# One layer of a streaming encoder on one core: the second copy of the band keys' upper half goes by DMA, and the last norm of the band rows stands behind two gate projections

## The chip, the core and the metric

The kernel runs on one core of one Trainium2 chip. The core has five engines, each with its own stream of instructions: TensorE (PE in the profile, with its weight loads as PEld), VectorE (DVE), ScalarE (ACT), GpSimd (POOL) and SyncE (SP), which here does nothing but issue DMAs. Engines wait for each other by semaphores. Matrix products are summed in PSUM, a small memory that PE writes and that DVE and ACT read out; all else lies in SBUF, a memory of 128 partitions, or in DRAM.

The metric is the device time of one execution, in microseconds (us). Lower is better.

## The reference

One layer is applied to a prompt of 1024 tokens and, with the same weights, to a sample of 32 tokens that has a cache of 512 older keys and values and a recurrent state. The change touches two things: how the keys of the band attention (branch B) are laid out before its scores, and when the last of its rows are divided by their softmax sums.

```python
h = rms_norm(x, g_pre_mix)
qa, ka, va, ra, alr, qb, kb, vb, ga, gb = split_cols(h @ w_in)
oa, s_gla = gla_branch(qa, ka, va, ra, alr, w_a2, b_a2, g_gla, gla_s0, gla_block)   # 4 linear heads
ob, k_rows, v_rows = attn_fn(qb, kb, vb, rel_bias)                                  # 8 band heads of 64
mix = (jax.nn.sigmoid(ga) * (oa @ w_br_a) + jax.nn.sigmoid(gb) * (ob @ w_br_b)) @ w_out
x = x + rms_norm(mix, g_post_mix)
f, conv_new = conv_ffn(rms_norm(x, g_pre_ffn), conv_s0, w_up, conv_w, conv_b, w_down)
x = x + rms_norm(f, g_post_ffn)
gate = jax.nn.sigmoid(rms_norm(x, g_pre_ple) @ w_ple_gate)
x = x + rms_norm(gate * (pe @ w_ple), g_post_ple)

def band_attend(q, k, v, q_pos, k_pos, rel_bias):
    s = jnp.einsum('bqhe,bkhe->bhqk', q, k).astype(jnp.float32) * HD_B ** -0.5
    ...
    s = jnp.where(vis, s + bias, -jnp.inf)
    p = jax.nn.softmax(s, axis=-1)
    return jnp.einsum('bhqk,bkhe->bqhe', p.astype(v.dtype), v)
```

## The kernel before

Activations are kept transposed: 128 features on the partitions, the 1056 tokens (prompt and sample together, `T`) along the free axis, cut into three chunks of 352. Everything is float32, but the products run on a rounded type (fp32r): each operand x is split into a rounded part (hi) and the rest (lo), and `product` adds three matmuls for each block of 128 features, hi weights by hi rows, hi weights by lo rows, lo weights by hi rows (L229, L230, L231). With eight blocks that makes 24 matmuls of 128 x 352 for one chunk of one projection.

**Weights.** `weights` loads 128 x 1024 numbers by one DMA on SP's queue (L199, tile `raw`, two buffers), ACT rounds each half (L208, `whi`, four buffers), and POOL subtracts (L209, `wlo`, four buffers). `project(n, evac)` loads one such block, runs the 24 matmuls for each of the three chunks in a PSUM tile `mm` (three buffers) and lets DVE read it out with the row scale (`to_tile`, L460). Full rows of 1056 go to tiles named `ev`, of which there are five for the whole kernel.

**Band attention.** The loop at L655 runs over four pairs of heads (`hp`). `band_project` projects Q, K and V of the pair, stores K and V, transposes V on PE (L505 and L510) and splits it. `band_head` then prepares one head of the two. A head has 64 features, and its q and k lie on partitions 0 to 63 or 64 to 127 of the pair's tile: `r` are the partitions it has, `o` the other 64. The score needs (q_hi + q_lo) by (k_hi + k_lo). The kernel does it with two matmuls over 128 partitions: `qs` holds q_hi on `r` and q_lo on `o`, `kh` holds k_hi on both halves and `kl` holds k_lo on both. So the halves `r` of `kh` and `kl` are made by ACT (L523, rounding) and DVE (L524, the rest), first for the 1056 new keys (`kf`), then for the 512 cached keys (`kc`), and each is then copied to the partitions `o` by L529: `kh` by POOL (`KHC` is 2) and `kl` by DVE (`KLC` is 0), 64 x 1568 numbers a copy. `probs` runs the two matmuls (L543 with `kh`, L544 with `kl`, PSUM tile `two`, one buffer), DVE adds the bias and finds the maximum (L550), ACT takes the exponential. The probabilities are transposed on PE (L559), split, and multiplied by V. The scores are written at high priority, so that the scheduler sets them ahead of projections.

After a pair its sums are inverted and stored to DRAM (`d_inv`, L678), the unnormed output rows too (`d_ob`, L684), and one projection of merge gates follows for pairs 0 to 2 (`gates`, which projects, takes the sigmoid and stores, L641).

**Norm.** `band_norm(hp)` loads the rows of a pair (L649), loads each head's inverses to 64 partitions (two DMAs, L651), multiplies on POOL (L652, 128 x 1056) and stores the result (L653). All four DMAs are on SP's queue. For pairs 0 to 2 it runs one pair later. For pair 3 it is called at L890, in the loop over the four linear heads.

**Linear heads.** `gla_project(h)` projects r, v, v, q, k of head 0, and q, k, v, v, r of the others. `gla_head` takes the decay of each token: a small product, ACT's exponentials, and nine scans on DVE (L786) over 128 tokens each. For each segment of 256 tokens DVE and ACT make seven scaled copies of q and k in a tile `x` (L807 is one of its operations), PE multiplies them (L835, PSUM tile `two`), DVE picks out the scores with masks (L840, L841), and PE applies them (L849). Then `gates(GLA_GATES[h])` projects two gates for head 0, 3, 2 and 6 for the others. The calls read

```python
for h in range(4):
    q, k, vt = gla_project(h)
    gla_head(h, q, k, vt)
    if h == 0:
        band_norm(3)
    gates(GLA_GATES[h])
```

**Order.** The code above is not the order in which the engines run it. The program is handed to a scheduler that plays the instructions through a timeline of its own and fixes for each engine the row in which they stand; what comes earlier in the code goes first where both could run, except for what is written at high priority (`weights`, the read-outs, the scores). Between such pieces, partial sums of the down weights (`d_s`, L430 on POOL's queue, L432 on SP's) are set in step by step. On each engine and in each DMA queue the instructions then run in that fixed row, and one that waits holds up all behind it.

Of the kernel before, what the change touches and what calls it, by code (L numbers as in the profile page):

```python
# [11 lines left out]
F32 = mybir.dt.float32  # L12
F32R = mybir.dt.float32r
U8 = mybir.dt.uint8
AF = mybir.ActivationFunctionType
ALU = mybir.AluOpType
# [6 lines left out]
T = NP + NS  # L23
# [34 lines left out]
GLA_GATES = (2, 3, 2, 6)  # L58
# [10 lines left out]
DVE_LO = (5,)  # L69
DVE_LO_O = (1, 3, 5, 7)  # L70
QSL = 2
KLL = 0
KLC = 0
NORM = 2
NORME = 0
KHC = 2
PSL = None
LOW_N = 50
LOW_G = 0
# [30 lines left out]
def emit(tc, a):  # L110
    nc = tc.nc
    ve, ac, po, pe, dma = nc.vector, nc.scalar, nc.gpsimd, nc.tensor, nc.sync
    uid = [0]
    E3 = (ve, ac, po)
# [5 lines left out]
    def pool(name, bufs=1, side="left"):  # L120
        return tc.alloc_tile_pool(name=name, bufs=bufs, side=side, reuse_waits="tile")

    def tl(p, shape, dt=F32, tag=None, bufs=None):
        tag = tag or nm("t")
        kw = {} if bufs is None else {"bufs": bufs}
        return p.tile(list(shape), dt, name=nm(tag), tag=tag, **kw)
# [31 lines left out]
    def evt():  # L158
        return tl(ev, [P, T], tag="ev", bufs=EVB)
# [287 lines left out]
    def project(n, evac):  # L447
        projects[0] += 1
        if projects[0] > 6:
            next(sums_left, None)  # L450
        hi, lo = weights(a["w_in"][n])
        for c in range(NC):
            s = chunk(c)
            ps = ps_mm()[:, : s.stop - s.start]
            product(ps, hi, lo, [(k, k) for k in range(KT)], lambda k: xh[:, k, s], lambda k: xl[:, k, s])
            with tc.high_priority():
                evac(ps, s)

    def to_tile(t):
        return lambda ps, s: ve.tensor_tensor(t[:, s], ps, rstd(s), op=ALU.mult)  # L460
# [54 lines left out]
    def band_head(hp, hd, qf, kf, kc, split, vs, ob, sums):  # L515
        r = slice(64 * hd, 64 * hd + 64)
        o = slice(64 - 64 * hd, 128 - 64 * hd)
        qs, kh, kl = split
        ac.activation(qs[r], qf[r], AF.Copy)
        E3[QSL].tensor_tensor(qs[o], qf[r], qs[r], op=ALU.subtract)  # L520

        for part, src in ((slice(0, T), kf), (slice(T, T + 512), kc)):
            ac.activation(kh[r, part], src[r], AF.Copy)  # L523
            E3[KLL].tensor_tensor(kl[r, part], src[r], kh[r, part], op=ALU.subtract)  # L524
        for e, t in ((KHC, kh), (KLC, kl)):
            if e == 1:
                ac.activation(t[o], t[r], AF.Copy)
            else:
                E3[e].tensor_copy(t[o], t[r])  # L529
        bias = tl(bp, [P, NS + 640], tag="bias", bufs=2)  # L530
        dma.dma_start(bias, a["rel"][2 * hp + hd])
        po.memset(bias[64:128, NS : NS + 64], NEG)
# [103 lines left out]
    def gates(cnt):  # L636
        for n, w0, dst in todo_gates[:cnt]:
            g = evt()
            project(w0 + n, to_tile(g))
            ac.activation(g, g, AF.Sigmoid)  # L640
            dma.dma_start(dst[n], g)  # L641
        del todo_gates[:cnt]
# [4 lines left out]
    def band_norm(hp):  # L647
        t, rb = evt(), evt()
        dma.dma_start(t, d_ob[hp])  # L649
        for hd in range(2):  # L650
            dma.dma_start(rb[64 * hd : 64 * hd + 64], d_inv[hp, hd, :T].partition_broadcast(64))  # L651
        po.tensor_tensor(t, t, rb, op=ALU.mult)  # L652
        dma.dma_start(d_on[hp], t)  # L653

    for hp in range(4):  # L655
        qf, kf, kc, split, vs = band_project(hp)
# [5 lines left out]
        for hd in range(2):  # L662
            po.memset(sums[hd], 1.0)
            work += band_head(hp, hd, qf, kf, kc, split[hd], vs, ob, sums[hd])
# [63 lines left out]
    def gla_project(h):  # L728
        q = tl(gp, [P, T], tag="qk", bufs=4)
        k = tl(gp, [P, T], tag="qk", bufs=4)  # L730
        vt = tl(gp, [P, 9, 256], tag="vt", bufs=2)
        vf = []
        for part in (ORD0 if h == 0 else ORD):
            if part == "q":
                project(Q0 + h, lambda ps, s: ve.scalar_tensor_tensor(q[:, s], ps, float(P ** -0.5), rstd(s), op0=ALU.mult, op1=ALU.mult))
            elif part == "k":
                project(K0 + h, to_tile(k))
            elif part == "r":
                gla_rest(h)
            elif part == "v":  # L740
                vf.append(evt())
                project(V0 + 2 * h + len(vf) - 1, to_tile(vf[-1]))
        for n in range(0, 9, 2):
            cnt = min(2, 9 - n)
            ps = ps_one()
            w = P if n < 8 else NS
            for i in range(cnt):
                for j in range(2):
                    pe.transpose(ps[:w, i * 256 + j * P : i * 256 + (j + 1) * P], vf[j][:, (n + i) * P : (n + i) * P + w], ident)
            ac.activation(vt[:w, n : n + cnt], ps[:w, : cnt * 256].rearrange("p (i v) -> p i v", v=256), AF.Copy)  # L750
        if 'r' not in (ORD0 if h == 0 else ORD):
            gla_rest(h)
        return q, k, vt
# [132 lines left out]
    for h in range(4):  # L886
        q, k, vt = gla_project(h)
        gla_head(h, q, k, vt)
        if h == 0:
            band_norm(3)  # L890
        gates(GLA_GATES[h])
    C0 = CHUNKS[0][1]
    b0 = [tl(gp, [P, 9 * 256], F32R, tag="vt", bufs=2)[:, : 4 * C0].rearrange("p (k t) -> p k t", t=C0)]
    b0 += [tl(gp, [P, T], F32R, tag="qk", bufs=4)[:, : 2 * C0].rearrange("p (k t) -> p k t", t=C0) for i in range(2)]
# [42 lines left out]
    op = pool("op")  # L937
    oa = [[tl(op, [P, T], F32R, tag=f"oa{kt}{x}") for x in "hl"] for kt in range(KT)]
    for kt in range(KT):
        t = evt()  # L940
# [18 lines left out]
    for n in range(KT):  # L959
        hi, lo = weights(a["w_br_a"][n])  # L960
        g, t = evt(), evt()
# [1118 lines left out]
```

## Time and profile before

| what | value |
|---|---|
| median of 3 runs | 1980.6 us (1978.6 to 1981.62) |
| profiled execution, its own time | 1979.3 us |
| span of that execution | 1977.6 us |
| mean granted clock of TensorE | 0.991 |
| PE busy, 0 to 60 us | 56.04 us |
| PE busy, 60 to 420 us (band heads) | 355.46 of 360 us |
| PE busy, 420 to 840 us (linear heads) | 411.99 of 420 us |
| PE busy, 840 to 1257 us | 406.36 of 417 us |
| PE busy, 1257 to 1640 us | 378.73 of 383 us |
| PE busy, 1640 to 1977 us | 317.18 of 337 us |
| copies of `kh`, POOL, L529 | 8, 2412 / 2508 / 2553 ns |
| casts of `kl`, DVE, L529 | 8, 1414 / 1762 / 3123 ns |
| norm multiplies, POOL, L652 | 4, 2462 / 2480 / 2696 ns |

The three numbers in the last rows are the shortest, the median and the longest. The span runs from the first to the last instruction; the execution's own time is 1.7 us longer. Between 60 and 840 us PE does something for all but 12.6 of 780 us. In the views that follow, a group of instructions has its engine, its line in the kernel before, the operation, what it writes and reads, and the tile's size. A number with `<-` in brackets is the idle time of the engine just before, and who ended it.

### The profile page before, as it was taken

The numbers are of one execution on the slowest core, as the hardware profiler recorded it, in microseconds if no ns is written. First come the engines' busy times: TensorE is split into PE (matmuls) and PEld (weight loads), VectorE is DVE, ScalarE is ACT, GpSimd is POOL, SyncE is SP. The second block draws the span as 40 slices with busy tenths as digits, with TensorE's granted clock in tenths as the row PEclk, the third lists the DMA queues.
The fourth block names the chain that finished last, engine by engine and source line by source line (L and its number), as shares of the span: only waits on it lengthen the run. The fifth ranks groups of instructions, "written<-read, shape, count | busy, mean of one in ns | idle before, by whom it ended". The sixth has DMA issues, their size and how long they took to land.

```text
span 1977.6 us, 34638 instructions
## 1 busy us (share of the span) xinstructions
PE 1925.8 (97%) x13584; PEld 1888.0 (95%) x13584; DVE 1260.6 (64%) x2500; ACT 943.2 (48%) x1706; POOL 462.5 (23%) x556
## 2 busy tenths in 40 slices
PE   9999999999999999999999999999999999999996
PEld 8999999999999999999999999999999999999996
DVE  6556556456366475466655677787777776456777
ACT  6356455455364463564434455333333445445444
POOL 2423333232112121211120111232122222115211
PEclk9999999999999999999999999999999999999998
DMA  7323345353444221226787247654334348556679
GB/s 265 100 86 121 100 132 143 99 147 104 113 146 115 81 66 60 97 87 236 255 291 241 89 160 232 218 180 137 130 128 138 123 162 306 183 185 200 202 233 222
DMA packets 107582, 312.04 MB, mean 158 GB/s; under 512 B 13268, under 2 KB 35612, under 8 KB 107292
## 3 DMA queue, kind: packets, MB, share of 16 engines
q1 hardware_dynamic: 81612, 222.99, 34.1%
q0 software_dynamic: 24976, 85.96, 14.6%
q8 instruction: 106, 1.74, 0.4%
q10 hardware_dynamic: 832, 0.90, 0.1%
q14 instruction: 56, 0.46, 0.1%
HBM read 226.34 MB, written 106.52 MB: 168 GB/s over the span
## 4 chain that ended last, share of the span: by engine, by line
PE 69%; DVE 11%; issue 10%; DMA 4%; ACT 4%; POOL 1%; SPq 0%; POOLq 0%; ACTq 0%; DVEq 0%
PE mm L230 10%; PE mm L229 10%; PE mm L231 10%; PE c L1527 7%; PE two L1312 6%; PE two L1313 6%; PE two L1314 6%; DMA hn<-d_hn 3%; PE aux L1527 2%; PE two L835 2%; PE one L601 2%; DVE z L1633 1%; PE one L559 1%; PE two L543 1%; PE one L849 1%
## 5 line engine op out<-in xcount | busy, mean ns | idle before, releaser
L231 PE MATMUL mm<-xh,wlo 128*128 128x352 f32 x1248 | 413.7, 331 | 0.0
L229 PE MATMUL mm<-xh,whi 128*128 128x352 f32 x1248 | 412.9, 331 | 0.0
L230 PE MATMUL mm<-xl,whi 128*128 128x352 f32 x1248 | 410.5, 329 | 0.0
L209 POOL TENSOR_TENSOR wlo<-raw,whi 128x512 fp32r<-128x512 f32 x128 | 181.0, 1418 | 686.8 <-ACT whi L208 630.5
L229 PEld LDWEIGHTS mm<-xh,whi 128*128 128x128 f32 x1248 | 236.1, 189 | 1.9 <-DVE ev L460 0.8
L230 PEld LDWEIGHTS mm<-xl,whi 128*128 128x128 f32 x1248 | 235.7, 189 | 1.7 <-issue 0.3
L231 PEld LDWEIGHTS mm<-xh,wlo 128*128 128x128 f32 x1248 | 235.5, 189 | 1.3
L1312 PE MATMUL two<-mh,whi 128*128 128x264 f32 x576 | 163.1, 287 | 5.8 <-ACT av L1193 2.4
L1314 PE MATMUL two<-mh,wlo 128*128 128x264 f32 x576 | 164.5, 287 | 0.0
L1313 PE MATMUL two<-ml,whi 128*128 128x264 f32 x576 | 164.2, 286 | 0.0
L208 ACT ACTIVATE whi<-raw 128x512 fp32r<-128x512 f32 x140 | 87.0, 628 | 149.7 <-PE mm L230 90.9
L1527 PE MATMUL c<-mh,wlo 128*128 128x264 f32 x438 | 124.5, 284 | 0.8 <-DMA wlo<-d_g 0.8
L1527 PE MATMUL c<-ml,whi 128*128 128x264 f32 x438 | 124.1, 283 | 0.9 <-DVE ml L1447 0.9
L1527 PE MATMUL c<-mh,whi 128*128 128x264 f32 x438 | 124.5, 284 | 0.0
L1312 PEld LDWEIGHTS two<-mh,whi 128*128 128x128 f32 x576 | 108.6, 190 | 6.7 <-ACT av L1193 2.7
L1314 PEld LDWEIGHTS two<-mh,wlo 128*128 128x128 f32 x576 | 109.8, 191 | 0.0
L1313 PEld LDWEIGHTS two<-ml,whi 128*128 128x128 f32 x576 | 109.7, 190 | 0.0
L460 DVE TENSOR_TENSOR ev<-mm,rstd 128x352 f32<-128x352 f32 x120 | 61.3, 519 | 50.4 <-PE mm L231 46.7
L1527 PEld LDWEIGHTS c<-mh,wlo 128*128 128x128 f32 x438 | 82.2, 188 | 1.5 <-DMA wlo<-d_g 1.5
L1527 PEld LDWEIGHTS c<-ml,whi 128*128 128x128 f32 x438 | 82.5, 188 | 1.1 <-DVE ml L1447 1.1
L1302 ACT ACTIVATE whi<-ws 128x512 fp32r<-128x512 f32 x72 | 45.3, 628 | 80.2 <-PE two L1313 48.1
L1527 PEld LDWEIGHTS c<-mh,whi 128*128 128x128 f32 x438 | 82.5, 188 | 0.0
(516 smaller groups left out, 5459.4 us busy)
## 6 DMA issues: line engine op xcount, KB each, us to landing
raw<-in_w_in SPq DMA_DIRECT2D x52, 512.0 KB, 3.7
uraw<-d_b POOLq DMA_DIRECT2D x34, 528.0 KB, 5.0
raw<-in_w_up SPq DMA_DIRECT2D x27, 512.0 KB, 3.6
hn<-d_hn SPq DMA_DIRECT2D x24, 528.0 KB, 4.9
d_b<-av POOLq DMA_DIRECT2D x44, 264.0 KB, 2.7
d_s<-in_w_down POOLq DMA_DIRECT2D x16, 704.0 KB, 7.9
draw<-d_s SPq DMA_DIRECT2D x16, 704.0 KB, 4.1
hn<-d_b POOLq DMA_DIRECT2D x40, 264.0 KB, 3.9
```

Of the source, the lines that this page charges most:

```text
L208: ac.activation(hi[-1][:, d], raw[:, b], AF.Copy)
L209: eng.tensor_tensor(lo[-1][:, d], raw[:, b], hi[-1][:, d], op=ALU.subtract)
L229: pe.matmul(ps, h, xh(kt), start=(first and i == 0), stop=False)
L230: pe.matmul(ps, h, xl(kt), start=False, stop=False)
L231: pe.matmul(ps, l, xh(kt), start=False, stop=(last and i == n - 1))
L460: return lambda ps, s: ve.tensor_tensor(t[:, s], ps, rstd(s), op=ALU.mult)
L601: pe.matmul(ps[:, j0 * P : j1 * P], vs[:, k, vd], got[x][:, k - kb, j0:j1], start=(i == 0 and x == "h"), stop=(i == len(work) - 1 and x == ...
L1302: ac.activation(h, x, AF.Copy)
L1312: pe.matmul(ps[:, j, :HC], w[0][:, k], x[0][:, k, s], start=st, stop=False, skip_group_check=True)
L1313: pe.matmul(ps[:, j, :HC], w[0][:, k], x[1][:, k, s], start=False, stop=False, skip_group_check=True)
L1314: pe.matmul(ps[:, j, :HC], w[1][:, k], x[0][:, k, s], start=False, stop=sp_, skip_group_check=True)
L1527: pe.matmul(ps, w, x, start=st, stop=sp_, skip_group_check=True)
```

## The change

Three constants go (`KLL`, `KLC`, `KHC`), and two places are written anew.

```diff
-        for part, src in ((slice(0, T), kf), (slice(T, T + 512), kc)):
+        for part, src in ((slice(T, T + 512), kc), (slice(0, T), kf)):
             ac.activation(kh[r, part], src[r], AF.Copy)
-            E3[KLL].tensor_tensor(kl[r, part], src[r], kh[r, part], op=ALU.subtract)
-        for e, t in ((KHC, kh), (KLC, kl)):
-            if e == 1:
-                ac.activation(t[o], t[r], AF.Copy)
-            else:
-                E3[e].tensor_copy(t[o], t[r])
+            dma.dma_start(kh[o, part].bitcast(F32), kh[r, part].bitcast(F32))
+            ve.tensor_tensor(kl[r, part], src[r], kh[r, part], op=ALU.subtract)
+        ve.tensor_copy(kl[o], kl[r])
...
     for h in range(4):
         q, k, vt = gla_project(h)
         gla_head(h, q, k, vt)
+        gates(GLA_GATES[h])
         if h == 0:
             band_norm(3)
-        gates(GLA_GATES[h])
```

In `band_head` the cached keys come first and the new keys second, and the copy of `kh` to the other 64 partitions is now two DMAs a head on SP's queue (64 x 512 and 64 x 1056 numbers, SBUF to SBUF) in place of one copy on POOL. Over eight heads that is sixteen DMAs for eight copies. The subtraction and the copy of `kl` stay on DVE. In the loop over the linear heads `band_norm(3)` comes behind the two gate projections of head 0.

The scheduler works out the rows anew, so they move elsewhere too. Names below are tiles with the numbers that the program gives them; lines in rows of the change are those of the changed kernel, which are 3 to 6 lower than in the kernel before.

SP's queue at the first pair, before: loads of cached keys and values (`kc`, `cv`), of the biases of both heads, then the stores of K (`out_o_kp`, `out_o_ks`) and the next weights (`raw`).

```order
L483 DMA kc_559<-in_cache_k 128x512
L511 DMA cv_854<-in_cache_v 128x512
L531 DMA bias_872<-in_rel 128x672
L531 DMA bias_885<-in_rel 128x672
L483 DMA kc_1428<-in_cache_k 128x512
L511 DMA cv_1724<-in_cache_v 128x512
L487 DMA out_o_kp<-ev_556 128x512
L488 DMA out_o_ks<-ev_556 128x32
L199 DMA raw_1518<-in_w_in 128x1024
```

And now, from the biases on:

```order
L525 DMA bias_887<-in_rel 128x672
L521 DMA kh_102_551<-kh_102_551 64x512
L521 DMA kh_105_554<-kh_105_554 64x512
L480 DMA kc_1430<-in_cache_k 128x512
L508 DMA cv_1726<-in_cache_v 128x512
L484 DMA out_o_kp<-ev_556 128x512
L485 DMA out_o_ks<-ev_556 128x32
L521 DMA kh_102_551<-kh_102_551 64x1056
L521 DMA kh_105_554<-kh_105_554 64x1056
L196 DMA raw_1520<-in_w_in 128x1024
```

The copies of the cached keys stand ahead of the next pair's loads, those of the new keys between the stores of K and the next weights.

PE where the first scores of the kernel stand (`two_889` of `kh` and `kl`), before. `mm_1339` is the first chunk of the first gate's projection, and V's transposes (L505) stand just ahead of it.

```order
L229 MATMUL mm_1339<-xh_135,whi_1331 128x352
L230 MATMUL mm_1339<-xl_136,whi_1331 128x352
L543 MATMUL two_889<-kh_102_551,qs_101_550 128x128
L544 MATMUL two_889<-kl_103_552,qs_101_550 128x128
L231 MATMUL mm_1339<-xh_135,wlo_1332 128x352
```

And now, in `mm_799`, the third chunk of V's own projection (L538 is the score's second matmul, with `kl`):

```order
L226 MATMUL mm_799<-xh_135,whi_739 128x352
L227 MATMUL mm_799<-xl_136,whi_739 128x352
L228 MATMUL mm_799<-xh_135,wlo_740 128x352
L538 MATMUL two_891<-kl_103_552,qs_101_550 128x128
L226 MATMUL mm_799<-xh_135,whi_743 128x352
L227 MATMUL mm_799<-xl_136,whi_743 128x352
L228 MATMUL mm_799<-xh_135,wlo_744 128x352
```

The first matmul, with `kh`, stands six projection matmuls ahead of these, that is behind the first six of the chunk's 24. Both have moved from behind V's transposes to ahead of them. DVE's read of that score (L550, now L544) has moved with them, from behind the read-out of V's third chunk to ahead of it.

POOL in linear head 0, before. The `wlo` are, two rows for each block of weights: the second gate of head 0 (raw_5286), then q (5380) and k (5469) of head 1; L652 is the norm's multiply.

```order
L209 TENSOR_TENSOR wlo_5289<-raw_5286,whi_5288 128x512
L209 TENSOR_TENSOR wlo_5293<-raw_5286,whi_5292 128x512
L652 TENSOR_TENSOR ev_5185<-ev_5185,ev_5186 128x1056
L430 DMA d_s_531<-in_w_down 128x1408
L209 TENSOR_TENSOR wlo_5383<-raw_5380,whi_5382 128x512
L209 TENSOR_TENSOR wlo_5387<-raw_5380,whi_5386 128x512
L209 TENSOR_TENSOR wlo_5472<-raw_5469,whi_5471 128x512
L209 TENSOR_TENSOR wlo_5476<-raw_5469,whi_5475 128x512
```

And now, with the multiply at L646 (the same blocks are raw_5287, raw_5388 and raw_5477):

```order
L206 TENSOR_TENSOR wlo_5290<-raw_5287,whi_5289 128x512
L206 TENSOR_TENSOR wlo_5294<-raw_5287,whi_5293 128x512
L206 TENSOR_TENSOR wlo_5391<-raw_5388,whi_5390 128x512
L206 TENSOR_TENSOR wlo_5395<-raw_5388,whi_5394 128x512
L206 TENSOR_TENSOR wlo_5480<-raw_5477,whi_5479 128x512
L646 TENSOR_TENSOR ev_5377<-ev_5377,ev_5378 128x1056
L206 TENSOR_TENSOR wlo_5484<-raw_5477,whi_5483 128x512
```

The multiply has moved three weight halves later, to between the halves of k's block of head 1. Of its DMAs, the load of the rows now stands ahead of the store of the first gate on SP, the two loads of the inverses behind it.

More of the change, by code (lines that the diff above doesn't have):

```diff
@@ L71 @@
 QSL = 2
-KLL = 0
-KLC = 0
 NORM = 2
 NORME = 0
-KHC = 2
 PSL = None
```

## The prediction

> **What bounds the kernel now.** The page's first part gives, for each engine, its busy time, its share of the span and its instructions.
>
> ```profile
> PE 1925.8 (97%) x13584; PEld 1888.0 (95%) x13584; DVE 1260.6 (64%) x2500; ACT 943.2 (48%) x1706; POOL 462.5 (23%) x556
> ```
>
> TensorE (PE) has work 97% of the time, and the change takes no matmul away. So it can gain only where PE stands idle, or where its clock is low. The table of waits shows who kept PE waiting: in us in total, times, and the longest. The first two rows are the whole answer for 60 to 420 us, the third the whole answer for 420 to 440 us.
>
> ```profile
> PE one L505 <- DVE ev L460: 2.4, 1, 2.4
> PE two L543 <- DVE sm L550: 1.9, 6, 0.4
> ```
>
> ```profile
> PE two L835 <- DVE x L807: 2.9, 1, 2.9
> ```
>
> The band heads and the start of the first linear head hold three kinds of wait: one of 2.4 us, one of 2.9 us, and six small ones. Next come stretches of 3.41 us: borders, length, PE busy (matmuls), granted clock, DMA share, GB/s.
>
> ```profile
> 79.43:82.85 3.42, 1.01 (x8) 1.00 0.06 25
> 82.85:86.26 3.41, 3.41 (x15) 0.50 0.68 168
> ...
> 431.00:434.42 3.42, 0.53 (x4) 1.00 0.80 158
> 434.42:437.83 3.41, 3.41 (x13) 0.50 0.85 270
> ...
> 1253.60:1257.00 3.40, 1.53 (x12) 1.00 0.64 206
> 1257.00:1260.40 3.40, 3.40 (x18) 0.50 0.74 242
> ...
> 1639.30:1642.70 3.40, 1.85 (x16) 1.00 0.77 207
> 1642.70:1646.10 3.40, 3.40 (x31) 1.00 0.77 246
> ```
>
> A stretch in which PE idles long enough is followed by one at half clock, which loses half of 3.41, **1.7 us**. Idle 1.87 us (3.40 - 1.53) was enough; idle 1.55 us (3.40 - 1.85) was not. So the first wait cost 2.4 + 1.7 = 4.1 us and the third 2.9 + 1.7 = 4.6 us. The Trainium skill, "TensorE: Matmul & The Clock Gate", Part 1, has the half rate come after at least one idle window of about 3.4 us. By that rule gaps of 2.4 and 2.9 us would cost no clock, and the sum below would be smaller by 3.4 us. The rows differ: 2.4 us of idle were followed by 0.50, so the sum goes by the rows.
>
> **Part 1: POOL's eight copies of the keys' upper half become sixteen DMAs.** The first wait is at the first pair of band heads. VectorE (DVE) and GpSimd (POOL) there, each row with start, length, engine, line, count and the idle time before:
>
> ```profile
> 73.85 3.72 DVE L524 TENSOR_TENSOR kl<-ev,kh 64x1056 fp32r<-64x1056 f32 x2 [1.16 <-ACT kh L523]
> 77.60 0.53 DVE L460 TENSOR_TENSOR ev<-mm,rstd 128x352 f32<-128x352 f32 x1
> 78.15 3.56 DVE L529 CAST kl<-kl 64x1568 fp32r<-64x1568 f32 x2
> 81.74 0.95 DVE L460 TENSOR_TENSOR ev<-mm,rstd 128x352 f32<-128x352 f32 x2
> ```
>
> ```profile
> 73.95 4.97 POOL L529 CAST kh<-kh 64x1568 fp32r<-64x1568 f32 x2 [0.54 <-ACT kh L523]
> 79.01 3.83 POOL L209 TENSOR_TENSOR wlo<-raw,whi 128x512 fp32r<-128x512 f32 x2
> ```
>
> ```profile
> L524 DVE TENSOR_TENSOR kl<-ev,kh x8: 1249/1254/2436, 73.8 to 307.7; 64x1056 fp32r<-64x1056 f32 x8
> ```
>
> ```profile
> L529 DVE CAST kl<-kl x8: 1414/1762/3123, 78.2 to 310.9; 64x1568 fp32r<-64x1568 f32 x8
> ```
>
> ```profile
> 79.36 0.32 PE L231 MATMUL mm<-xh,wlo 128*128 128x352 f32 x1
> 79.53 0.38 PE L505 MATMUL one<-ident,ev 128*128 128x128 f32 x2
> 82.32 0.55 PE L505 MATMUL one<-ident,ev 128*128 128x128 f32 x3 [2.41 <-DVE ev L460]
> ```
>
> PE wants to transpose V, but the second third of V leaves PSUM only at 81.74 (L460), behind four DVE operations on the keys. One of the two subtractions took 2.44 us instead of 1.25 while POOL copied beside it: 1.19 us. POOL's next weights (79.01) waited for its copies and then ran beside DVE's second cast. With POOL's copies gone DVE should be through with the casts at about 81.7 - 1.2 - 0.4 = 80.1 (78.15 + 3.56 = 81.7; the casts 1.4 and 1.8 us, the shortest and the median, instead of 3.56 together). PE had nothing to do from 79.9 on, so little of the 2.41 would be left by this alone.
>
> The new order changes what PE waits for. The first scores (L543 and L544) now stand 6 and 12 matmuls into V's last third, and need the DMA copy and then the cast. That is the wait the change adds: behind it on PE are 18 projection matmuls and V's transposes, and for those waits everybody. PE gets there after 6 of 24 matmuls. The last of the 24 begins at 79.36, and they follow each other at 0.16 us, so the first begins at 75.7 and the score at **76.6**.
>
> When does the copy land? ScalarE (ACT) ends the rounded keys of head 0 after half of this row, at 73.8, and SP is free then:
>
> ```profile
> 72.73 2.20 ACT L523 ACTIVATE kh<-ev 64x1056 fp32r<-64x1056 f32 x2 [3.23 <-DVE ev L460]
> ```
>
> ```profile
> out_o_kp<-ev SPq DMA_DIRECT2D x1, 256.0 KB, 3.5
> ```
>
> ```profile
> ev<-d_inv SPq DMA_DIRECT2D x8, 264.0 KB, 9.9
> ```
>
> The trace has no transfer from SBUF to SBUF. The nearest rows: the store of 256 KB just ahead of the copy in the same queue took 3.5 us to land. The only transfers over 64 partitions, 264 KB like the copy's, took 9.9 us, but each pair is queued behind the load of a whole pair's rows, and reads one DRAM row 64 times. By these the copy (64 x 1056 floats, 264 KB) lands between 73.9 + 3.5 = 77.4 and 73.9 + 9.9 = 83.8; it may also land sooner, as its target is not DRAM, and from 76.6 down that costs nothing. I take 3.7 us, near the first row: **77.6**, a wait of 1.0 us. The Trainium skill, "SBUF — State Buffer", on the port swizzle, says that 64 partitions get no more DMA bandwidth than 32, at most some 218 GB/s beside 2 us fixed: an estimate from that page of 2 + 270 KB / 218 GB/s = 3.2 us. This speaks against the change's form, and by it the wait would be 0.5 us and the sum 0.5 us better. No run here shows such a copy yet.
>
> After 77.6: 6 matmuls, 78.6; the cast for L544 ends about 78.2 and is no longer late; 12 more, 80.7; V's second third is out at 80.1 to 80.6. So 2.41 us of idle turn into 1.0 us in one stretch, too little for the clock: 2.41 - 1.0 + 1.7 = **3.1 us gained**. Ends: 4.1 (the copy lands before PE asks) and nothing (it lands after 78.2, with the idle over 1.55).
>
> For the other pairs the copy is no bound: its keys are ready 15 us or more before their first use, since tiles are free only when the head before is done with them. What goes there is the small wait at the first heads of pairs 1 to 3:
>
> ```profile
> 162.54 0.39 PE L543 MATMUL two<-kh,qs 128*128 128x256 f32 x1 [0.37 <-DVE sm L550]
> ```
>
> ```profile
> 159.03 3.12 DVE L529 CAST kl<-kl 64x1568 fp32r<-64x1568 f32 x1
> ```
>
> The cast takes 3.12 us there instead of 1.4, beside POOL's copy and its subtraction. Without the copy DVE is some 2 us earlier: 3 x 0.37 = **1.1 us gained**; the other three of the six (1.9 - 1.1 = 0.8 us together) stay. Against this, pair 1 in its new order has 7 projection matmuls between V's transposes and the heads' transposes instead of 13: 6 x 0.16 = 0.97 us of cover less, of which I charge **0.4 us** (ends 0 and 0.97).
>
> On SP, what stands behind each copy are the bias, outputs and weights. Each copy waits for an ACT split, and the bias load next to it already waits as long for DVE. I cost this at nothing; the cover is the two weight buffers.
>
> **Part 2: the last pair's rows are normed behind two gate projections.** Now the third wait:
>
> ```profile
> 423.44 6.79 DVE L786 TENSOR_TENSOR_SCAN b<-ev,ev 128x128 f32<-128x128 f32 x9 [1.73 <-ACT ev L783]
> ```
>
> ```profile
> L786 DVE TENSOR_TENSOR_SCAN b<-ev,ev x36: 194/400/2640, 423.4 to 833.1; 128x128 f32<-128x128 f32 x32, 128x32 f32<-128x32 f32 x4
> ```
>
> ```profile
> 424.39 2.70 POOL L652 TENSOR_TENSOR ev<-ev,ev 128x1056 f32<-128x1056 f32 x1 [12.27 <-DMA ev<-d_inv]
> 427.02 0.86 POOL L430 DMA_DIRECT2D d_s<-in_w_down  x1
> 427.65 1.55 POOL L209 TENSOR_TENSOR wlo<-raw,whi 128x512 fp32r<-128x512 f32 x1
> ```
>
> A scan takes 0.40 us, but the worst 2.64: it ran beside POOL's norm multiply (L652). Moving the multiply gives DVE back 2.64 - 0.40 = 2.24 us. POOL's weights (L209) still fall on the scans. PE's 2.89 us become 0.65, below the clock's limit: 2.24 + 1.7 = 3.9 us at this place. What is late next is the first segment's scores:
>
> ```profile
> 448.10 1.02 DVE L841 COPY_PREDICATED scores<-masks,two 128x64 f32<-128x64 uint8 x4
> ```
>
> ```profile
> 449.94 0.61 PE L849 MATMUL one<-scores,vt 128*128 128x128 f32 x4
> ```
>
> DVE is 0.8 us ahead of PE here (449.1 against 449.9). PE comes 3.9 us earlier, DVE 2.24: 3.9 - 2.24 - 0.8 = 0.85 us are lost again. **3.1 us gained** (ends: 4.6, and nothing if a new idle brings the clock down again).
>
> The moved step issues four DMAs and the multiply. On SP its last two loads now stand behind the first gate's store, on POOL the multiply stands between the halves of the second head's k weights:
>
> ```profile
> 435.78 0.32 SPq L641 DMA_DIRECT2D d_gb<-ev  x1
> ```
>
> ```profile
> 441.71 4.01 POOL L209 TENSOR_TENSOR wlo<-raw,whi 128x512 fp32r<-128x512 f32 x2 [8.08 <-ACT whi L208]
> ```
>
> Issued at about 436, with 9.9 us to land, the loads let the multiply start at about 446. That is where DVE, 2.24 us earlier and with one of these two weight halves beside it instead of both, should end L841 (446 to 446.9); I take it that they miss each other. The multiply ends at 449. The half behind it is used after q's last third has left PSUM:
>
> ```profile
> 457.06 0.52 DVE L735 SCALAR_TENSOR_TENSOR qk<-mm,rstd 128x352 f32<-128x352 f32 x1 [2.03 <-PE mm L231]
> ```
>
> Even 4 us earlier that leaves it some 3 us. The store of the normed rows waits on SP with the v weights behind it, and those are used later still.
>
> **Sum.** -3.1 - 3.1 - 1.1 + 0.4 = -6.9 us. The profiled execution took 1979.3 us (span 1977.6 and 1.7 around it), so **1972.4 us**. The median of the runs, 1980.6, is 1.3 above that execution.
>
> **Rivals.**
> - **One of the two waits comes back.** The copy lands after 78.2, the idle passes 1.6 us, and part 1's 3.1 are gone: 1975.5. Or the moved multiply falls on DVE's operations ahead of L841: 2.2 us of stall, the new idle at L849 is over 1.6 us, and part 2's 3.1 are gone: also 1975.5. For the one: 3.7 us is an estimate; against it, SP has nothing else to issue at 73.9. For the other: 446 against 446 to 446.9 is close; against it, a stalled multiply or weight half would cost DVE one operation's delay only.
> - **Both come back, or POOL was never what held DVE.** Then only 1.1 - 0.4 are left: 1978.6. Against it: the two lengths of L524 and of L786, which have no other reason in the rows.
> - **Slower: the copy takes as long as the other 64-partition loads or longer.** At 9.9 us PE stands from 76.6 to 83.8 and pays the clock: 7.2 against 2.4 us, +4.8; with the other terms, +1.0, 1980.3. It decides from 9 us on, and at 13 us it is 1983.4. For it: the only rows of 64 partitions. Against it: their queue.
>
> **Numbers.** Chances: both waits shrink 0.58; one comes back 0.24; both 0.10; slower copy 0.08. The range reaches from a gain of 9.8 (4.1 + 4.6 + 1.1), 1969.5, less 1.0 since the repeats of the kernel before lie 3 us apart, 1968.5, to 1979.0, where both have come back. A measurement of this kernel can tell about 0.2%, 4 us. Faster by more than that: 0.56 of the first case and half of the second, 0.69; within: 0.23; slower: 0.08.
>
> **What would show it.** Right: no wait of PE at L505 over 1 us, one of 0 to 1.5 us at the first L543, clock 1.00 after both places; POOL without copies; L524 at 1.25 us for both heads; scans with one long one instead of two; L835 waiting under 1 us. Wrong: a copy landing later than 4.3 us after its issue, a half clock within 76 to 90 or 430 to 455 us, or a new wait at L849 for L841.

## The result, and the profile after

| | median | runs | ratio to before, 95% interval |
|---|---|---|---|
| before | 1980.6 us | 5 | |
| changed kernel | 1971.08 us (1968.61 to 1973.84) | 5 | 0.9956 [0.9942, 0.9969] |

The changed kernel is faster by 0.3 to 0.6%; the forecast was 1972.4. Two more sets of runs further down put it at 0.9980 [0.9968, 0.9993] and 0.9958 [0.9942, 0.9975], so the gain lies between 0.1 and 0.6%; the mean of the three is 0.35%. (The ratios are not quite the quotients of the medians.) The profiled execution took 1971.22 us, its span 1969.5.

The page's first part, changed kernel:

```profile
PE 1922.2 (98%) x13584; PEld 1886.2 (96%) x13584; DVE 1254.0 (64%) x2500; ACT 943.8 (48%) x1706; POOL 440.5 (22%) x548
```

POOL has eight instructions and 22 us less; PE has the same matmuls. Next, the changed kernel's table of waits of PE (us in total, times, the longest), first for 60 to 420 us, then for 420 to 460 us:

```profile
PE two L537 <- DMA kh<-kh: 1.0, 1, 1.0
PE two L537 <- DVE sm L544: 0.7, 3, 0.2
...
PE one L843 <- DVE scores L835: 2.3, 1, 2.3
```

The wait at V's transposes (2.4 us) is gone, and the change's own wait, for the copy, has come in its place with 1.0 us. Of the six small waits three are left at 0.2 us each. The longest scan takes 1.47 us in place of 2.64, and the wait at the first linear head's scores (L835 before, 2.9 us) is gone too, but one of 2.3 us has come a little later, at the product that uses the masked scores (L843, before L849). The stretches of the clock at both places, changed kernel (PE, PEld, DVE, ACT and POOL busy, granted clock, DMA share, GB/s):

```profile
75.03:78.45 3.42, 2.45 (x16) 2.19 (x16) 3.30 (x6) 0.56 (x1) 0.00 (x0) 1.00 0.93 270
78.45:81.86 3.41, 3.41 (x25) 3.39 (x24) 1.36 (x6) 1.77 (x6) 2.49 (x2) 1.00 0.61 244
436.89:440.30 3.41, 1.75 (x11) 1.45 (x9) 3.38 (x7) 3.37 (x7) 2.23 (x2) 1.00 1.17 330
440.30:443.72 3.42, 2.80 (x23) 2.80 (x24) 1.32 (x6) 0.79 (x4) 0.00 (x0) 1.00 0.35 117
...
901.06:904.47 3.41, 2.08 (x17) 1.97 (x17) 0.06 (x1) 0.65 (x2) 1.27 (x1) 1.00 0.98 278
904.47:907.88 3.41, 2.61 (x9) 2.61 (x10) 1.78 (x4) 0.00 (x0) 0.00 (x0) 0.50 1.03 420
907.88:911.29 3.41, 3.41 (x14) 3.23 (x13) 0.82 (x2) 1.43 (x3) 0.00 (x0) 0.50 0.98 354
```

Both places run at full clock now. The wait of 2.3 us near 439 us fell on the border of two stretches (1.66 us of idle in one, 0.62 in the next), and neither brought the clock down. Two stretches near 905 us are at half clock, where the kernel before had none. Just before them PE idled 1.33 us of a stretch, less than the 1.55 that the prediction took as harmless.

**A ledger by place.** Two spans can't be compared place by place when their matmuls stand in another order. So I took for each matmul the time to the next one's start, less the median of that time for the same line and operands over all profiled kernels, and summed it by stretch (times of the kernel before; other kernels at the same amount of work done). What a stretch shows is PE's idle time, its restarts and its half clock. The level of a column depends on the count: with the matmuls that come sooner than their median counted against the others, 100 to 340 us has some 7 us less in every row. The differences between two kernels stay within 0.5 us, so read those. All profiled executions, in us:

```
kernel              1-70  70-100  100-340  340-415  415-460  880-925  rest
before              8.00    5.40    16.00     3.17     5.12     3.88  53.2
before, again       7.36    5.24    15.99     3.16     6.19     3.62  50.4
change              6.90    1.77    13.29     3.17     3.32     7.72  50.3
change, again       7.88    2.17    13.27     3.17     3.34     7.18  47.9
change, third       8.14    1.85    13.29     3.17     3.30     5.56  52.4
copy alone          6.96    1.71    13.27     3.17     4.17     6.50  57.5
norm alone          6.24    3.85    16.00     3.17     6.47     6.30  49.8
copy on ScalarE     7.86    0.54    16.27     3.09     5.03     5.68  53.2
copy on POOL, parts 8.07    2.63    17.05     3.17     4.77     3.41  50.5
new keys in two     5.22    2.43    15.00     3.17     3.22     7.95  53.8
norm a head later   7.54    2.19    13.29     3.17     1.52     8.35  51.1
queries off POOL    8.30    1.99    20.54     3.17     4.82     6.34  53.3
candidate           7.00    0.55    13.33     3.17     1.54     6.77  47.8
candidate, queries  7.54    0.53    19.98     3.16     1.51     8.14  48.4
```

From 70 to 460 us, where the change lies, the kernel before loses 29.7 and 30.6 us and the changed one 21.6, 22.0 and 21.6: a gain of 8 to 9. The stretches from 70 to 415 us repeat to 0.4 us. The rest, in which PE's row is the same in all kernels, does not: "rest" alone runs from 47.8 to 57.5 us, for the same code. So single runs of one kernel differ by several us, and the stretch from 880 to 925 us takes 1.7 to 4.1 us of the gain back in all three profiles of the changed kernel.

### The profile page after: what moved, and what is told of

Same layout as the page of the kernel before. It is cut to its first block, busy times and chain, and to the rows that moved or that the text cites. A ratio compares the mean times of both kernels' runs of the same rounds, so it can differ in the third digit from the quotient of the medians.

```text
span 1969.5 us, 34671 instructions
## 1 busy us (share of the span) xinstructions
PE 1922.2 (98%) x13584; PEld 1886.2 (96%) x13584; DVE 1254.0 (64%) x2500; ACT 943.8 (48%) x1706; POOL 440.5 (22%) x548
## 4 chain that ended last, share of the span: by engine, by line
PE 71%; DVE 15%; ACT 6%; DMA 6%; issue 3%; SPq 0%; POOL 0%; ACTq 0%; DVEq 0%; POOLq 0%
PE mm L226 11%; PE mm L228 11%; PE mm L227 11%; PE c L1521 7%; PE two L1306 6%; PE two L1307 6%; PE two L1308 6%; DMA hn<-d_hn 2%; PE aux L1521 2%; PE one L595 2%; PE two L829 2%; PE one L553 1%; DVE z L1627 1%; DVE d L797 1%; DVE z L1055 1%
## 5 line engine op out<-in xcount | busy, mean ns | idle before, releaser
L457 DVE TENSOR_TENSOR ev<-mm,rstd 128x352 f32<-128x352 f32 x120 | 61.4, 518 | 51.6 <-PE mm L228 50.0
L557 DVE TENSOR_TENSOR pt<-one,pt 128x128 fp32r<-128x128 f32 (+3 forms) x96 | 46.7, 498 | 57.4 <-ACT pt L556 57.3
```

What stands on the lines that cost most here:

```text
L557: ve.tensor_tensor(out[1], tv, out[0], op=ALU.subtract)
```

## The experiments

All times in one table, then what each was for. The expectations use an earlier count of the ledger, over fewer kernels and with other borders, that is lower by some 0.9 us from 100 to 340 us. Before had medians of 1978.59, 1978.3 and 1978.07 us (24 to 29 runs) beside the three groups.

| kernel | median | runs | ratio to before |
|---|---|---|---|
| 1 copy alone | 1972.3 | 12 | 0.9966 [0.9953, 0.9978] |
| 2 norm alone | 1976.12 | 12 | 0.9989 [0.9975, 1.0003] |
| 3 change, again | 1972.78 | 12 | 0.9980 [0.9968, 0.9993] |
| 4 before, again | 1976.92 | 1 | |
| 5 copy on ScalarE | 1973.56 | 12 | 0.9971 [0.9959, 0.9984] |
| 6 copy on POOL, in parts | 1974.09 | 12 | 0.9983 [0.9970, 0.9995] |
| 7 new keys in two | 1976.6 | 12 | 0.9993 [0.9980, 1.0005] |
| 8 norm a head later | 1970.39 | 6 | 0.9956 [0.9939, 0.9974] |
| 9 queries off POOL | 1980.7 | 12 | 1.0015 [1.0005, 1.0025] |
| 10 candidate | 1971.07 | 7 | 0.9961 [0.9945, 0.9976] |
| 11 candidate, queries off POOL | 1975.19 | 12 | 0.9985 [0.9975, 0.9995] |
| 12 change, third time | 1971.54 | 6 | 0.9958 [0.9942, 0.9975] |

**1 and 2: each part alone.** The copy alone is the changed kernel with the norm's call put back; the norm alone is the kernel before with this one edit:

```diff
     for h in range(4):
         q, k, vt = gla_project(h)
         gla_head(h, q, k, vt)
+        gates(GLA_GATES[h])
         if h == 0:
             band_norm(3)
-        gates(GLA_GATES[h])
```

> Part 1 alone: the copies of the keys' upper half go by DMA, the last norm stands where it stood before. My theory (each place gains by itself, by what POOL no longer does beside VectorE there): the changed kernel's ledger of TensorE time by place shows 3.9 us gained at the first pair and 2.4 us over the three later pairs, so about 6.3 us less than before, 1974.3; the wait of the first linear head's scores for x is back at 2 to 3 us with a half clock behind it, and the first pair waits 0.8 to 1.2 us for the copy. Rival 1 (the gain of the later pairs came from the whole program's new order): less than 4.5 us gained here. Rival 2 (what the changed kernel gained and lost from 900 us on is part of the change): the losses near 905 and 1057 us and the gain at 1253 to 1290 us are here as in the changed kernel.

> Part 2 alone: the last norm behind the two gate projections, the copies on POOL as before. My theory: 1.8 us less than before (4.6 of wait and clock gone, 2.3 to 2.8 come back as a wait for the masked scores), 1978.8; the first pair keeps its wait of 2.4 us at V's transposes with a half clock behind. Rival 1 (the norm's move was worth the 3.1 us that I predicted): 1977.5. Rival 2 (the multiply moved onto VectorE's path again gives all back): 1980 to 1981, no change.

The copy alone gains all of the change's band stretches (1.71 and 13.27 in the ledger) and 0.34% in time; rival 1 is out. The wait of the first linear head is back with 2.6 us, but without the half clock that was expected behind it: it lay on a border (1.8 and 0.8 us). The norm alone gains nothing that its stretch shows (6.47 against 5.12 and 6.19), and its time is not told from no change. Its waits of PE, at the two places:

```profile
PE one L505 <- DVE ev L460: 2.4, 1, 2.4
...
PE one L849 <- DVE scores L841: 2.2, 1, 2.2
```

The first row is the old wait at V's transposes, the second the same new one as in the changed kernel. Each meets the clock otherwise than there. The stretches at both, norm alone:

```profile
76.33:79.74 3.41, 1.82 (x12) 1.56 (x11) 3.35 (x3) 0.84 (x2) 3.33 (x3) 1.00 0.39 160
79.74:83.16 3.42, 2.58 (x18) 2.58 (x19) 2.15 (x7) 1.07 (x4) 1.36 (x1) 1.00 0.35 89
83.16:86.57 3.41, 3.41 (x25) 3.37 (x24) 1.27 (x5) 1.15 (x6) 0.00 (x0) 1.00 0.48 151
...
441.56:444.97 3.41, 1.17 (x8) 0.88 (x7) 3.31 (x10) 2.74 (x6) 1.35 (x1) 1.00 1.35 370
444.97:448.39 3.42, 3.42 (x19) 3.42 (x18) 0.10 (x1) 0.55 (x2) 0.00 (x0) 0.50 0.43 176
```

The wait of 2.4 us, followed by a half clock in both profiles of the kernel before, lies here on a border (1.59 and 0.84 us) and costs no clock. The wait of 2.2 us, free of it in the changed kernel, lies here within one stretch and costs two stretches at half clock (6.8 us long, to 451.8). So what a wait of this size costs is settled by where the stretches begin, and that differs from run to run.

**3, 4 and 12: both kernels again, unchanged.**

> The changed kernel once more, unchanged, for a second look at its places. If the steps from 900 us on are chance (when a DMA lands against the clock's windows), then some of them are absent here: the half clock near 905 us (worth 3.8 us), the wait for weights near 1057 us (2.1 us), the missing half clock near 1257 us. If they belong to the change they are all here within 0.5 us. The first pair's wait for the copy should be 0.8 to 1.2 us, the wait for the masked scores near 438 us 2.0 to 2.6 us in either case. Time 1968.5 to 1974.

> The kernel before once more, unchanged, for a second look at the same places. The waits at V's transposes (2.4 us) and at the first linear head's scores (2.9 us), each with a half clock behind, should be here within 0.3 us, as they come from the order of the rows. The half clocks near 1257 and 1291 us and the two windows at the start may be absent if they are chance. Time 1977 to 1982.

> The changed kernel, unchanged, on the same chip as the candidates. The wait for the copy at the first score 0.8 to 1.4 us, the wait for the masked scores 2.0 to 2.6 us, with a half clock behind it only if about 1.9 us or more of the idle time fall into one of the clock's windows; time 1969 to 1975.

The waits came back as expected: 1.4 and 1.0 us for the copy, 2.3 and 2.2 for the masked scores; 2.4 and 2.7 in the kernel before. The loss near 1057 us (2.0 in the first profile) was gone in the second and back in the third, and the losses from 1245 to 1310 us, half clocks above all, vary in both kernels (10.06 and 5.21 us there before, 5.94, 4.40 and 5.98 after): they come and go with no change to the kernel. The loss near 905 us came back in all three. PE waits there for a product with a gate's rows, and those for their load:

```profile
PE mm L226 <- DVE ev L922: 1.9, 1, 1.9
```

The first such product starts 5.5 us after its load's issue in both profiles of the kernel before, 6.5, 6.0 and 6.0 in the changed one. It is later with each part alone too, 6.7 with the copy and 6.2 with the norm, but 4.9 with the copies on POOL in parts. So the loss came with the change each time, and with either half of it; why the load takes longer was not settled.

**5 and 6: the same copies on another engine.** In place of the DMA:

```diff
-            dma.dma_start(kh[o, part].bitcast(F32), kh[r, part].bitcast(F32))
+            ac.activation(kh[o, part], kh[r, part], AF.Copy)
```

and in run 6, in the same place,

```diff
+            po.tensor_copy(kh[o, part], kh[r, part])
```

> The changed kernel with ScalarE making the sixteen copies in place of the DMAs (same parts, same order in the code). My theory, that what counts is POOL's absence beside VectorE: the three later pairs lose as little as in the changed kernel (12.4 us of TensorE time over nominal from 100 to 340 us, against 15.1 in the kernel before), the subtractions stay at 1.25 us, and the first pair loses its wait of 0.9 to 1.4 us for the copy: ScalarE needs 2.2 us more and ends by 76.1, TensorE asks at about 76. So 0 to 1 us faster than the changed kernel, if 16 copies (13.7 us of ScalarE) fall beside other work. Rival: ScalarE's row is what the pairs wait for (exponentials, splits of the probabilities), then the later pairs lose 1 us or more each and the kernel is slower than the change by 3 us or more.

> The changed kernel with POOL making the sixteen copies in place of the DMAs: new order of the parts, and the norm's new place, but POOL beside VectorE again. My theory: the gains of the band pairs are gone, 14.5 to 15.5 us over nominal from 100 to 340 us as before and 4.5 to 5.5 from 70 to 100 us (with a half clock; 3.5 to 4 without), subtractions of 2.4 us again; 5 to 6 us slower than the changed kernel. Rival (the new order of the parts, cached keys first, gave the gain): within 1.5 us of the changed kernel.

On ScalarE the first pair has no wait at all (0.54), as expected, but the later pairs gain nothing (16.27): the rival holds there. PE's waits from 100 to 415 us:

```profile
PE one L553 <- ACT pt L556: 0.7, 2, 0.4
PE one L553 <- DVE vs L497: 0.6, 2, 0.3
PE one L553 <- ACT whi L205: 0.4, 1, 0.4
```

ScalarE, with 13.7 us more, is late with V's and the probabilities' splits. With POOL in the new order the sum was as expected, 27.6 us lost from 70 to 460 us, 6 more than in the changed kernel (the ratios to before, 0.9983 and 0.9980, don't show it), but not where expected. The first pair waits 1.0 us at V's transposes again, and still loses only 2.63 us, nearer to the changed kernel (1.77 to 2.17) than to the norm alone, which has no half clock there either (3.85). Pair 1 loses 3.5 us, but pairs 2 and 3 together come out within 0.4 us of the changed kernel. So in pairs 2 and 3 the new order with the copy in two parts (cached keys first) does most of it, in the first pair more than half of what is not the clock's, and not POOL's absence. What its absence would do in the old order no run shows. Pair 1's loss is a wait for V's split:

```profile
PE one L553 <- DVE vs L497: 1.5, 1, 1.5
```

**7: the copy issued earlier.**

```diff
-        for part, src in ((slice(T, T + 512), kc), (slice(0, T), kf)):
-            ac.activation(kh[r, part], src[r], AF.Copy)
+        C2 = CHUNKS[1][1]
+        for part, src in ((slice(T, T + 512), kc), (slice(0, C2), kf), (slice(C2, T), kf)):
+            x = src[r] if src is kc else src[r, part]
+            ac.activation(kh[r, part], x, AF.Copy)
```

(`C2` is 704; the subtraction takes `x` in the same way.)

> The changed kernel with the new keys copied in two parts (the first 704, then 352), so that the first score needs only a copy issued some 4 us earlier. My theory (the one new wait of the change is the copy's landing, 3.7 us after its issue): TensorE does not wait at the first score, 1.0 to 1.4 us less at 70 to 100 us, the rest as in the changed kernel. Rival: eight more DMAs and eight more operations each on ScalarE and VectorE make VectorE late with the casts, and the wait moves to the score with kl or to V's transposes, no gain. Within 1.5 us of the changed kernel in either case; the profile decides, not the time.

```profile
72.70 0.30 PE L539 MATMUL two<-kh,qs 128*128 128x128 f32 x1 [1.63 <-DMA kh<-kh]
```

Neither held. The scheduler saw the score's operands come earlier and set the score earlier, into the second chunk of V: it waits 1.6 us for the copy in place of 1.0. The later pairs lose 1.7 us as well (15.00 in the ledger; five small waits, 1.7 us, where the changed kernel has three). A wait for a DMA does not go away by issuing it earlier, if the reader is moved with it.

**8: the norm one head later.**

```diff
-        if h == 0:
+        if h == 1:
             band_norm(3)
```

> The changed kernel with the last norm one linear head later still (behind the gates of head 1). My theory, that the moved multiply fell on VectorE just ahead of the masked scores and made the wait of 2.3 us near 439 us: that wait falls below 1 us (one weight half on POOL stays there), 1.3 us or more less over nominal from 415 to 460 us (3.3 in the changed kernel), and a stall of one scan or product appears in head 1 (near 575 us) of which 0 to 1.5 us reach TensorE. Rival (the wait for the masked scores is set by VectorE's own row, not by POOL): it stays at 2 us or more.

```profile
PE one L843 <- DVE scores L835: 0.5, 1, 0.5
```

The wait fell from 2.3 to 0.5 us and the stretch from 3.3 to 1.52, while 460 to 880 us rose by 0.3. POOL's multiply was the cause.

**9: the queries' subtraction off POOL.** Pairs 1 to 3:

```diff
-        E3[QSL].tensor_tensor(qs[o], qf[r], qs[r], op=ALU.subtract)
+        (ve if hp else E3[QSL]).tensor_tensor(qs[o], qf[r], qs[r], op=ALU.subtract)
```

> The changed kernel with the queries' subtraction of pairs 1 to 3 (qs, 64 x 1056) on VectorE in place of POOL. It tests why one cast in each of these pairs still takes 3.1 us although POOL copies nothing now: the trace shows POOL's subtraction for the queries beside it. My theory: the three long casts fall to 1.0 us, VectorE does the subtraction in about 1.25 us, so it is about 0.9 us earlier at the first scores of the next pair, and the small waits left there (0.2 us each) go; 0 to 1 us less over nominal from 100 to 340 us (12.4 in the changed kernel). Rival (the cast is slow for another reason, such as ScalarE or the DMAs): casts of 3 us stay, and VectorE is 1.25 us later, 1 us more or worse.

The casts there (shortest, median, longest), and PE's wait in pair 1:

```profile
L523 DVE CAST kl<-kl x8: 968/972/2060, 77.3 to 312.4; 64x1568 fp32r<-64x1568 f32 x8
```

```profile
PE one L553 <- DVE vs L497: 2.8, 2, 2.6
```

The cause is right, the use of it is not. The casts of 3.1 us are gone (2.06 at most, in the changed kernel 3.14), but VectorE is late elsewhere, with V's split in pair 1: a wait of 2.6 us, two stretches at half clock, and the kernel is slower than before.

**10 and 11: what beats the change by place.**

```diff
+            if hp == 0:
+                ac.activation(kh[o, part], kh[r, part], AF.Copy)
+            else:
+                dma.dma_start(kh[o, part].bitcast(F32), kh[r, part].bitcast(F32))
...
-        if h == 0:
+        if h == 1:
             band_norm(3)
```

> Candidate to beat both: the changed kernel with the first pair's four copies on ScalarE (no DMA to wait for), the other pairs' by DMA, and the last norm one linear head later. If places add up: 1.2 to 1.6 us less at 70 to 100 us, 1.8 us less at 415 to 460 us, nothing lost at the later pairs, so 3 us less than the changed kernel in its median, about 1969 against 1972. If the waits are only displaced (ScalarE's row late at V's split in the first pair, the norm's multiply on another head's products): within 1 us of the changed kernel.

> The candidate with the queries' subtraction of pairs 1 to 3 on VectorE too. If the three edits add up: 0 to 1 us less than the candidate. If VectorE's added 7.5 us come onto the path: 1 us or more slower than the candidate.

By place the edits add up: from 70 to 460 us the candidate loses 18.6 us against 21.6 of the change (0.55 + 13.33 + 3.17 + 1.54), and its profiled execution, 1964.64, is the fastest of the profiled ones. But its median, 1971.07, is that of the change on the same chip, 1971.54, within what the runs' scatter can tell. It beats the kernel before and is not shown to beat the change. With the queries' subtraction on VectorE it is 4 us slower.

## Why the prediction held, point by point

**The first pair: right, to 0.5 us.** The prediction had the copy land 3.7 us after its issue, and PE wait 1.0 us. The changed kernel's timeline (start, length, engine, line):

```profile
72.74 1.57 SPq L521 DMA_DIRECT2D kh<-kh  x2
72.75 2.54 DVE L522 TENSOR_TENSOR kl<-ev,kh 64x1056 fp32r<-64x1056 f32 x2 [1.15 <-ACT kh L520]
...
75.87 1.98 DVE L523 CAST kl<-kl 64x1568 fp32r<-64x1568 f32 x2
...
76.64 0.30 PE L537 MATMUL two<-kh,qs 128*128 128x128 f32 x1 [0.97 <-DMA kh<-kh]
```

Issue at 72.74, landing 3.8 us later, score at 76.64 after 0.97 us of waiting. The trace has the landing of eight of the sixteen copies: 2.2, 3.9 and 5.3 us (shortest, median, longest). So one was later than the 4.3 us that the prediction named as a sign of being wrong, but PE waited for the first alone. The slower rival (9.9 us) is out. The estimate of 3.2 us that the prediction worked out from the Trainium skill, "SBUF — State Buffer", on the port swizzle, was 0.7 below that median. The subtractions are at 1.25 us each, as expected, and the two casts at 0.99, not at the 1.4 and 1.8 taken. The gain is 3.1 to 3.6 us by the ledger, where 3.1 was forecast. Of it 1.5 us are the half clock, which the kernel with the norm alone escaped by chance (3.85 against 5.40 with the same wait). So that part of the sum was a probability, and I had counted it as certain. And run 6 shows that the remaining 1.7 to 2.1 us are not POOL's absence alone: with POOL copying in parts some 1.2 of them are there.

**The later pairs: right in sign, mis-sized by 2 us.** Forecast -1.1 + 0.4 = -0.7 us, measured 13.3 - 16.0 = -2.7. The term that was mis-sized is this, and its reason is wrong in part: "The cast takes 3.12 us there instead of 1.4, beside POOL's copy and its subtraction. Without the copy DVE is some 2 us earlier". The cast is as long as before; the changed kernel's DVE, and then POOL, at pair 1:

```profile
150.75 0.71 DVE L544 CUSTOM_DVE_ANT_0 s<-two,bias 32x544 f32<-32x544 f32 x1
...
151.50 0.79 DVE L522 TENSOR_TENSOR kl<-kc,kh 64x512 fp32r<-64x512 f32 x1
152.22 1.25 DVE L522 TENSOR_TENSOR kl<-ev,kh 64x1056 fp32r<-64x1056 f32 x1
153.50 3.14 DVE L523 CAST kl<-kl 64x1568 fp32r<-64x1568 f32 x1
```

```profile
153.15 2.66 POOL L517 TENSOR_TENSOR qs<-ev,qs 64x1056 fp32r<-64x1056 f32 x1 [1.40 <-ACT qs L516]
```

It is POOL's subtraction for the queries that holds it, as run 9 showed, and that stayed. What went is the stretching of another operation, the subtraction of the cached keys, 0.79 us here. In the kernel before, POOL and then DVE:

```profile
155.89 2.55 POOL L529 CAST kh<-kh 64x1568 fp32r<-64x1568 f32 x1 [1.37 <-PE one L559]
158.41 2.90 POOL L520 TENSOR_TENSOR qs<-ev,qs 64x1056 fp32r<-64x1056 f32 x1
```

```profile
154.29 0.71 DVE L550 CUSTOM_DVE_ANT_0 s<-two,bias 32x544 f32<-32x544 f32 x1 [0.20 <-PE two L544]
...
157.01 1.99 DVE L524 TENSOR_TENSOR kl<-kc,kh 64x512 fp32r<-64x512 f32 x1
159.03 3.12 DVE L529 CAST kl<-kl 64x1568 fp32r<-64x1568 f32 x1
```

The subtraction lies beside POOL's copy, the cast beside POOL's subtraction. That is worth 1.2 us here and 1.3 in pairs 2 and 3. Counted from DVE's read of the scores just ahead (L550, now L544, the first rows above), the cast ended after 7.9 us in each pair and now ends after 5.9, 6.4 and 6.4: DVE is 2.0 us earlier in pair 1 and 1.4 in the others. In pair 1 the other 0.8 us are a read-out of PSUM that moved ahead of these operations. In run 6, where POOL still copies, the cast ends after 7.0 us, and that 0.9 us was enough: the first waits of the three pairs are gone there too. So POOL's absence was not needed for these waits to go. The forecast priced these three waits at their idle time, 0.37 us each; measured, a wait of 0.37 us costs 0.53 (0.70 us between two starts where 0.16 is usual), 1.6 us for the three. A late start of the first score after 100 us, 0.3 us, is gone as well. The 0.4 us charged for less cover in pair 1 show up nowhere. The remaining 0.8 us of the 2.7 were not taken apart.

**The first linear head: the mechanism of a rival, the size of neither.** Forecast -3.1 us; the ledger has 3.3 after 5.12 and 6.19, so -1.8 to -2.9. The step that failed here is "Issued at about 436, with 9.9 us to land, the loads let the multiply start at about 446 [...] I take it that they miss each other". The changed kernel's POOL, and then DVE, just ahead of the masked scores:

```profile
435.21 2.49 POOL L646 TENSOR_TENSOR ev<-ev,ev 128x1056 f32<-128x1056 f32 x1 [0.98 <-DMA ev<-d_inv]
437.66 1.46 POOL L206 TENSOR_TENSOR wlo<-raw,whi 128x512 fp32r<-128x512 f32 x1
```

```profile
435.74 2.24 DVE L797 TENSOR_TENSOR d<-b 128x256 f32<-128x256 f32 x1
437.90 1.36 DVE L800 TENSOR_TENSOR x<-d,qk 128x128 f32<-128x128 f32 x1
439.19 0.28 DVE L801 TENSOR_TENSOR x<-d,qk 128x128 f32<-128x128 f32 x1
```

The changed kernel is some 10 us earlier here (L835 masks the first scores of this segment at 433.00, L841 before at 443.05), and so are the loads, forecast at about 436 and issued at 426.63 and 427.74; the first of them landed after 7.7 us, not 9.9. So the multiply met DVE three operations ahead of the scores. The operation of 0.41 us took 2.24, the next one 1.36 in place of 0.28 beside the weight half: 2.9 us, which PE saw as 2.3. The rival had this stall and its price (2.2 us), and added a half clock that didn't come: in three profiles of the change and in run 7 the idle time lay on a border, in runs 2, 5, 6 and 9 a half clock followed. A new wait at this product was one of the prediction's own signs of being wrong.

**The sum.** -6.9 us were forecast. By place it was -8 to -9 from 70 to 460 us, of which the stretch near 905 us, nowhere in the prediction, took 1.7 to 4.1 back. The medians came out 9.5, 5.8 and 6.5 us below those of before, and 1972.4 lies between the changed kernel's three medians. That the total fits so well is in part luck, two errors that cancel: the later pairs gave 2 us more than forecast, and the stretch near 905 us took 1.7 to 4.1.

## What to carry to other kernels

When one engine's operation is stretched, look for which operation of the other engine lies beside it by its start and end, before giving the price to the one that the change removes: here two of POOL's operations lay beside VectorE's, and the change took only one away. A wait just large enough for the clock is to be priced with a probability, since a wait of 2.2 to 2.9 us was followed by none, one or two stretches at half clock. And where runs scatter by several us in untouched code, compare kernels stretch by stretch: a gain of 3 us in one place was clear there and did not show in a median.

## What was not expected of the hardware

**Some operations of VectorE and POOL exclude each other.** The stretched operations wait for POOL's to end. L797 ends at 437.98, 0.28 us after POOL's multiply (437.70), and takes 0.41 by itself; L800 at 439.26, 0.14 after the weight half (439.12), by itself 0.28; the cast at 156.64, 0.84 after POOL's subtraction (155.80), by itself 0.97. So each ends 0.13 to 0.14 us short of POOL's end and its own length together. DVE's read-out from PSUM (L457), at 435.31 beside the same multiply, took its usual 0.51 us. The Trainium skill, "SBUF — State Buffer", on the two separate sides of SBUF, has it so: VectorE and GpSimd share a pair of ports by an exclusive lock, which VectorE needs in its two-port modes and, beside an operation of GpSimd that reads SBUF, for two inputs in SBUF; it is held for a whole instruction, and whoever comes second waits for its end. The trace agrees, and by this rule the stall of 2.24 us could have been worked out ahead from the length of the multiply.

**The clock's stretches.** Idle time of 1.9 us or more within one stretch of 3.41 us was followed by a half clock in every profile, at the places of this change (1.91 to 2.89 us, eight cases). Waits of 2.2 to 2.6 us that lay on a border, at most 1.8 us to a side, had none in six cases; two more (at most 1.4 us to a side, runs 6 and 9) had one, and so had the stretches near 905 us in seven profiles, after 1.1 to 1.4 us of idle time (1.33 in the first profile of the change). So below 1.9 us idle time alone doesn't decide, and the prediction's limit of 1.55 us was no limit. Sometimes two stretches follow, sometimes one. The Trainium skill, "TensorE: Matmul & The Clock Gate", Part 1, has the half rate come after at least one idle window of about 3.4 us; by the trace none of the eight was idle for a whole window.
